# Sum transfers at intervals of their own in each stage, and the first wide layer's second product swept over 26 tiles

## The chip, the cores and the metric

One core of a Trainium2 chip runs the whole kernel. The metric is the device time of one execution in microseconds. The engines are TensorE (PE; its weight loads are shown apart as PEld), VectorE (DVE), ScalarE (ACT), GpSimd (POOL) and SyncE (SP), which issues most transfers.

## What is computed

Two residual layers over 512 tokens of width 1024, in float32, each an attention and then a wide layer (a squared-ReLU MLP with 4096 hidden columns):

```python
def sq_relu_mlp(h, w_up, w_down):
    u = jax.nn.relu(h @ w_up)
    return (u * u) @ w_down

for layer in range(2):
    hn = rmsnorm(h, norm_mix[layer])
    if layer % 2 == 0:
        h = h + hybrid_attention(hn, ...)        # 8 heads GQA and 8 heads MLA, softmax over 512 tokens
    else:
        h = h + neighbourhood_attention(hn, ...) # 16 heads over a window of 8 x 16 tokens
    h = h + sq_relu_mlp(rmsnorm(h, norm_ffn[layer]), ffn_w_up[layer], ffn_w_down[layer])
return rmsnorm(h, final_norm)
```

## The kernel before

Activations stand transposed: hT holds 8 tiles of 128 features by 512 tokens. Every matrix product is made as three products of a high and a low part (hi x hi, hi x lo, lo x hi), so each weight chunk is loaded (raw), its high part made on ScalarE (whi, L236 or L336 or L1340) and its low part as a difference on VectorE (wlo, L226 or L337 or L1341), before TensorE can use it.

The hidden width of a wide layer is 32 tiles of 128. They are treated in three groups, by the constants FIRST, RAW, MORE = 6, 22, 4:

- The first 6 tiles are made by a plain product (`plain`, matmuls of 512 columns on L545 to L547), and their part of the second product is plain too (`gens`).
- The other 26 are made by block products (class `Seven`, L416 to L418): two by two, with seven instead of eight half-size products of 256 columns. The sums of weight blocks that this needs are made on POOL (L329 to L331).
- Of those 26, 22 go on to the second product in the same block form, in three sweeps over 11 pairs of tiles (class `Sweeps`, L1443 to L1445, 256 columns). The last pair or two run as a tail, bank by bank, and the sums are added into hT on VectorE (L1449).
- The last 4 (MORE) are split and used in a plain product at the end (L545 to L547, and in the first layer L1519 for the additions into hT); in the second layer this end also makes the kernel's output.

The sweeps need sums of blocks of w_down. These are made ahead of time in DRAM by transfers alone (class `SumsAhead`): for each pair two copies of 512 KB issued by ScalarE (L841), and four adds of 256 KB issued by POOL (L832), each add a transfer that accumulates into the copy. `steps` yields after each transfer. A small pacemaker sets their place in the program: `tick(us)` is called with the nominal time of each matmul group and each attention step, and whenever `beat["every"]` of it has passed, one more transfer is written into the program. At the end of the block products `drain` writes what is left. `beat` is set when each attention begins to make the sums for the wide layer behind it (in the first attention at its step 22), and held until that layer's block products end.

The order of instructions on an engine is the scheduler's, from the program's order and its own model of times; the second attention alone (`fixed_order`) is in the written order. SP's loads go ahead as far as their buffers are free. In the wide layers one of the raw buffers is `shared`, which the attentions use for their softmax rows.

After the first wide layer the second attention begins: hT is scaled and split tile by tile (`split_g`: L551 on ScalarE, L552 on VectorE), its squares are summed (L559, L561), and TensorE makes the first group of values (`valuesC`, L1657 to L1659: four chunks of tokens, first over hT tiles 0 to 3, then over 4 to 7) and the first queries and keys (`projC`, L545 to L547). The column sums for the norm (L566) and the chain of small operations behind them (L568 to L1584) come beside these.

`bias_rows` writes the position bias of the second attention to DRAM by SP transfers; a step of it stands at every fourth matmul group of the later sweeps.

## Time and profile before

| | us |
|---|---|
| median of three runs | 1173.42 |
| lowest and highest | 1171.39, 1175.44 |
| the profiled execution | 1173.18 |
| its span, first to last instruction | 1171.4 |
| TensorE busy in the span | 1144.9 |

The stages in the trace, on its own time scale from the span's start: the first attention until about 253, its output product to 275, the first wide layer's plain part to about 365, its block products to 467, its sweeps to 578, its plain end to 600, the second attention and its products to about 815, the second wide layer from there to the end (block products to about 1025). A row of a view that groups by stage gives the busy time of each engine in that stretch; the length less TensorE's time is TensorE's idle time. In a row of waits stand the engine, the tile and line that waited, the one waited for, and the total, the count and the longest. In the chain of work that ended last a row is a start, a length and what it was.

### The profile page before, as it was taken

How to read it: one execution, taken by the hardware profiler on the slowest of the kernel's cores; microseconds unless marked ns; L12 is line 12 of the kernel's file. 1: busy time of each engine (PE TensorE's matmuls, PEld its weight loads, DVE VectorE, ACT ScalarE, POOL GpSimd, SP SyncE). 2: the span in 40 equal slices, each digit the busy share in tenths (PEclk: the TensorE clock that was granted, in tenths of full speed). 3: DMA queues.
4: the chain of work that ended last, by engine and by line, in shares of the span. 5: the costliest groups of instructions: out<-in, count | busy, mean ns of one | idle time of the engine just before them, and what ended most of it. 6: DMA issues, size and time to landing. Idle time of an engine off the chain costs nothing.

```text
span 1171.4 us, 20855 instructions
## 1 busy us (share of the span) xinstructions
PE 1144.9 (98%) x7596; PEld 1029.6 (88%) x7596; DVE 919.4 (78%) x1617; ACT 668.2 (57%) x1147; POOL 463.6 (40%) x486
## 2 busy tenths in 40 slices
PE   9989999999999999999999999999999999999996
PEld 8667778888799999999988998988788999999995
DVE  5788988778978787998474676767896878799845
ACT  5468576664536656756253555645552665675625
POOL 3267253333668795000002243333185898600000
PEclk9999999999999999999999999999999999999999
DMA  7123467664577666768426497778566666765702
GB/s 273 55 79 84 122 147 202 176 143 129 114 172 196 162 149 198 234 215 278 131 82 163 131 247 190 191 189 209 178 128 183 170 166 158 193 208 174 249 2 72
DMA packets 129543, 191.55 MB, mean 164 GB/s; under 512 B 12659, under 2 KB 81184, under 8 KB 128736
## 3 DMA queue, kind: packets, MB, share of 16 engines
q1 hardware_dynamic: 112304, 136.61, 37.1%
q0 software_dynamic: 14976, 29.38, 15.5%
q10 hardware_dynamic: 2160, 24.22, 6.2%
q8 instruction: 60, 0.98, 0.4%
q14 instruction: 43, 0.35, 0.1%
HBM read 167.75 MB, written 52.43 MB: 188 GB/s over the span
## 4 chain that ended last, share of the span: by engine, by line
PE 79%; DVE 10%; DMA 4%; ACT 3%; issue 2%; POOL 1%; SPq 0%; DVEq 0%; POOLq 0%; ACTq 0%
PE mm L547 7%; PE mm L545 7%; PE mm L546 7%; PE t L1444 3%; PE t L1443 2%; PE t L1445 2%; PE mm L418 2%; PE mm L416 2%; PE mm L417 2%; PE s L1070 2%; PE o L1058 2%; PE mm L1445 2%; PE mm L1443 2%; PE mm L1444 2%; PE t L1045 2%
## 5 line engine op out<-in xcount | busy, mean ns | idle before, releaser
L545 PE MATMUL mm<-a,whi 128*128 128x512 f32 x407 | 164.8, 407 | 0.3 <-ACT whi L236 0.2
L547 PE MATMUL mm<-a,wlo 128*128 128x512 f32 x407 | 160.2, 395 | 1.6 <-DVE wlo L226 1.5
L546 PE MATMUL mm<-a,whi 128*128 128x512 f32 x407 | 160.9, 395 | 0.1
L337 DVE TENSOR_TENSOR wlo<-raw,whi 128x896 fp32r<-128x896 f32 x80 | 110.5, 1388 | 28.6 <-ACT whi L336 28.4
L236 ACT ACTIVATE whi<-raw 128x1024 fp32r<-128x1024 f32 (+3 forms) x86 | 80.4, 939 | 86.4 <-PE s L546 29.7
L226 DVE TENSOR_TENSOR wlo<-raw,whi 128x1024 fp32r<-128x1024 f32 (+4 forms) x83 | 99.2, 1197 | 36.1 <-ACT whi L236 34.4
L336 ACT ACTIVATE whi<-raw 128x896 fp32r<-128x896 f32 x80 | 75.4, 949 | 83.6 <-PE o L546 22.9
L547 PEld LDWEIGHTS mm<-a,wlo 128*128 128x128 f32 x407 | 76.4, 188 | 19.4 <-DVE wlo L226 3.0
L545 PEld LDWEIGHTS mm<-a,whi 128*128 128x128 f32 x407 | 76.5, 188 | 16.1 <-ACT whi L236 1.3
L546 PEld LDWEIGHTS mm<-a,whi 128*128 128x128 f32 x407 | 76.8, 189 | 14.1 <-DVE a L903 0.4
L1609 POOL DMA_DIRECT2D a<-a x16 | 8.7, 545 | 185.7 <-PE mm L546 169.2
L1078 POOL TENSOR_SCALAR shared<-shared,ti 128x512 f32<-128x512 f32 x64 | 48.3, 758 | 84.5 <-DVE ti L1077 53.5
L418 PE MATMUL mm<-a,wlo 128*128 128x256 f32 x280 | 78.8, 282 | 0.7 <-DVE wlo L337 0.7
L417 PE MATMUL mm<-a,whi 128*128 128x256 f32 x280 | 78.5, 280 | 0.0
L416 PE MATMUL mm<-a,whi 128*128 128x256 f32 x280 | 78.4, 280 | 0.0
L1444 PE MATMUL t<-a,whi 128*128 128x256 f32 x264 | 74.2, 281 | 0.6 <-DVE a L1389 0.5
L1443 PE MATMUL t<-a,whi 128*128 128x256 f32 x264 | 73.9, 280 | 0.0
L1445 PE MATMUL t<-a,wlo 128*128 128x256 f32 x264 | 73.9, 280 | 0.0
L1701 POOL TENSOR_SCALAR shared<-shared,ti 128x256 f32<-128x256 f32 x64 | 35.5, 566 | 95.9 <-DVE ti L1700 83.6
L330 POOL TENSOR_TENSOR raw<-raw 128x512 f32<-128x512 f32 x40 | 67.8, 1695 | 3.1
L1341 DVE TENSOR_TENSOR wlo<-a,whi 128x1024 fp32r<-128x1024 f32 x42 | 51.1, 1221 | 19.4 <-ACT whi L1340 19.4
L329 POOL TENSOR_TENSOR raw<-raw 128x256 f32<-128x256 f32 x40 | 45.1, 1127 | 44.0 <-DMA raw<-in_ffn_w_up_dram 26.1
(399 smaller groups left out, 4007.3 us busy)
## 6 DMA issues: line engine op xcount, KB each, us to landing
made<-in_ffn_w_down_dram ACTq DMA_DIRECT2D x44, 512.0 KB
raw<-in_ffn_w_up_dram SPq DMA_DIRECT2D x80, 256.0 KB
a<-made SPq DMA_DIRECT2D x70, 256.0 KB
made<-in_ffn_w_down_dram POOLq DMA_DIRECT2D x44, 256.0 KB, 6.1
made<-made POOLq DMA_DIRECT2D x44, 256.0 KB, 6.8
raw<-in_ffn_w_down_dram SPq DMA_DIRECT2D x36, 256.0 KB
raw<-in_ffn_w_down_dram SPq DMA_DIRECT2D x16, 512.0 KB
raw<-in_od_w_qkv_dram SPq DMA_DIRECT2D x64, 128.0 KB
```

The source lines that it names most:

```text
L226: z = lambda: (eng or DVE).tensor_tensor(to, src, f32(high), op=ALU.subtract)
L236: ACT.activation(hi[:, 0:m], raw[:, 0:m], AF.Copy)
L337: DVE.tensor_tensor(lo[:, 0:896], raw[:, 128:1024], f32(hi[:, 0:896]), op=ALU.subtract)
L416: PE.matmul(o, wh, x[:, 0], start=kp == 0 and n in (0, 1, 3, 5), stop=False, skip_group_check=True)
L417: PE.matmul(o, wh, x[:, 1], start=False, stop=False, skip_group_check=True)
L418: PE.matmul(o, wl, x[:, 0], start=False, stop=kp == self.np - 1, skip_group_check=True)
L545: PE.matmul(o, wh, xh, start=first, stop=False)
L546: PE.matmul(o, wh, xl, start=False, stop=False)
L547: PE.matmul(o, wl, xh, start=False, stop=last)
L1443: PE.matmul(o, wh, x[:, 0], start=first and m % 2 == 0, stop=False, skip_group_check=True)
L1444: PE.matmul(o, wh, x[:, 1], start=False, stop=False, skip_group_check=True)
L1445: PE.matmul(o, wl, x[:, 0], start=False, stop=last, skip_group_check=True)
```

## The change

Four things:

- RAW and MORE are given per layer: in the first wide layer 26 and 0, in the second 22 and 4 as before. The first layer's second product is thus 6 plain tiles and three sweeps over 13 pairs, and has no plain end; the sums of two more pairs are made ahead for it (52 adds and 26 copies, in place of 44 and 22).
- The interval of the sum transfers was 4.2 from the first attention to the end of the first layer's block products, and 4.4 for the second. It is now 2.8 in the first attention, 3.3 in the plain part of the first wide layer and 5.4 beside its block products; 3.2, 3.6 and 7.0 for the second.
- A step of the bias rows stands at every fifth matmul group of the sweeps, in place of every fourth.
- Where there are no MORE tiles, no product for them is planned.

```diff
-    FIRST, RAW, MORE = 6, 22, 4
+    FIRST, RAW, MORE = 6, (26, 22), (0, 4)
...
-            beat.update(every=4.2, work=ahead0.steps())
+            beat.update(every=2.8, work=ahead0.steps())
...
-    ahead0, ahead1 = (SumsAhead(ins["ffn_w_down"][l], FIRST, RAW // 2) for l in range(2))
+    ahead0, ahead1 = (SumsAhead(ins["ffn_w_down"][l], FIRST, RAW[l] // 2) for l in range(2))
...
         wide[0], LOAD[0] = 4, 7
+        beat["every"] = (3.3, 3.6)[l]
...
         reserve[0] = 3
+        beat["every"] = (5.4, 7.0)[l]
         sweeps = []

-        R = stage(0, RAW + MORE, 0, lambda: sweeps.append(Sweeps(w, FIRST, made)))[1]
-        R, more = R[: RAW // 2], R[RAW // 2 :]
-        V = [Slot() for _ in range(MORE)]
+        R = stage(0, RAW[l] + MORE[l], 0, lambda: sweeps.append(Sweeps(w, FIRST, made)))[1]
+        R, more = R[: RAW[l] // 2], R[RAW[l] // 2 :]
+        V = [Slot() for _ in range(MORE[l])]
...
-            gens = [product(w, FIRST + RAW, up, tiles(512 * c, 512), lambda j, b, c=c: ev(4 * c + j, b))
-                    for c in range(2)]
+            gens = [product(w, FIRST + RAW[l], up, tiles(512 * c, 512), lambda j, b, c=c: ev(4 * c + j, b))
+                    for c in range(2) if up]
...
-            if kind and n % 4 == 0:
+            if kind and n % 5 == 0:
                 next(bias, None)
...
-    beat.update(every=4.4, work=ahead1.steps(), rest=True)
+    beat.update(every=3.2, work=ahead1.steps(), rest=True)
```

The lines behind the edits are numbered one or two higher in the changed kernel (L1657 becomes L1659, L1701 L1703).

Where the transfers stand by the order of the two programs, as copies on ScalarE and adds on POOL:

| | before | now |
|---|---|---|
| first attention (copies before ScalarE's last softmax row, adds before POOL's last one) | 12, 13 | 16, 20 |
| adds beside the first layer's block products | 23 | 20 |
| second attention (likewise) | 10, 13 | 14, 18 |
| adds beside the second layer's block products | 23 | 15 |

TensorE at the end of the first wide layer, before: the last rows of the plain end (o is a bank, a_905 and a_906 are hidden tiles), then the first values of the second attention (a_1081 is the split hT tile 0).

```order
L545 MATMUL o_1080_6750<-a_905_5215,whi_1075_6715 128x512
L546 MATMUL o_1080_6750<-a_905_5215,whi_1075_6715 128x512
L547 MATMUL o_1080_6750<-a_905_5215,wlo_1076_6716 128x512
L545 MATMUL o_1080_6750<-a_906_5216,whi_1075_6715 128x512
L546 MATMUL o_1080_6750<-a_906_5216,whi_1075_6715 128x512
L547 MATMUL o_1080_6750<-a_906_5216,wlo_1076_6716 128x512
L1657 MATMUL s_1090_6828<-whi_1093_6841,a_1081_6803 128x256
L1658 MATMUL s_1090_6828<-wlo_1094_6842,a_1081_6803 128x256
```

The same engine now, where the first values chunk (whi_1105) ends and the second (whi_1107) begins, 48 rows behind the last sweep matmul (a_1096 is hT tile 3, a_1097 tile 4).

```order
L1659 MATMUL s_1102_6954<-whi_1105_6967,a_1096_6932 128x256
L1660 MATMUL s_1102_6954<-wlo_1106_6968,a_1096_6932 128x256
L1661 MATMUL s_1102_6954<-whi_1105_6967,a_1096_6932 128x256
L1659 MATMUL o_1101_6953<-whi_1107_6971,a_1097_6933 128x256
L1659 MATMUL s_1102_6954<-whi_1107_6971,a_1097_6933 128x256
L545 MATMUL mm_1133_7147<-a_1093_6929,whi_1109_6975 128x512
L1660 MATMUL o_1101_6953<-wlo_1108_6972,a_1097_6933 128x256
L1661 MATMUL o_1101_6953<-whi_1107_6971,a_1097_6933 128x256
```

The sweeps' last matmul is now followed directly by the values; the scheduler has pulled one high product each of the other bank and of the first keys (mm_1133) ahead of the first use of wlo_1108.

VectorE at the same place before, from the plain end's last additions into hT (L1519) on; the low parts of the values' weights (L226) stand between them.

```order
L226 TENSOR_TENSOR wlo_1096_6846<-raw_1091_6830,whi_1095_6845 128x1024
L1519 TENSOR_TENSOR hT_74<-hT_74,s_1077_6747 128x512
L1519 TENSOR_TENSOR hT_74<-hT_74,t_1078_6748 128x512
L552 SCALAR_TENSOR_TENSOR a_1085_6807<-hT_74,gT_75,a_1085_6807 128x512
L1519 TENSOR_TENSOR hT_74<-hT_74,t_1079_6749 128x512
L552 SCALAR_TENSOR_TENSOR a_1086_6808<-hT_74,gT_75,a_1086_6808 128x512
L561 TENSOR_TENSOR shared_72<-shared_72,sc_1102_6872 128x512
L1519 TENSOR_TENSOR hT_74<-hT_74,o_1080_6750 128x512
L552 SCALAR_TENSOR_TENSOR a_1087_6809<-hT_74,gT_75,a_1087_6809 128x512
L226 TENSOR_TENSOR wlo_1098_6850<-raw_1091_6830,whi_1097_6849 128x1024
```

And now, from the sweeps' last additions into hT (L1449, bank t_908) on.

```order
L1449 TENSOR_TENSOR hT_74<-hT_74,o_910_5232 128x2x256
L552 SCALAR_TENSOR_TENSOR a_1097_6933<-hT_74,gT_75,a_1097_6933 128x512
L1449 TENSOR_TENSOR hT_74<-hT_74,t_908_5230 128x2x256 x2
L552 SCALAR_TENSOR_TENSOR a_1095_6931<-hT_74,gT_75,a_1095_6931 128x512
L552 SCALAR_TENSOR_TENSOR a_1096_6932<-hT_74,gT_75,a_1096_6932 128x512
L552 SCALAR_TENSOR_TENSOR a_1098_6934<-hT_74,gT_75,a_1098_6934 128x512
L552 SCALAR_TENSOR_TENSOR a_1099_6935<-hT_74,gT_75,a_1099_6935 128x512
L552 SCALAR_TENSOR_TENSOR a_1100_6936<-hT_74,gT_75,a_1100_6936 128x512
L226 TENSOR_TENSOR wlo_1108_6972<-raw_1103_6956,whi_1107_6971 128x1024
L226 TENSOR_TENSOR wlo_1110_6976<-raw_1103_6956,whi_1109_6975 128x1024
L561 TENSOR_TENSOR shared_72<-shared_72,sc_1112_6992 128x512
```

The low part of the second values chunk stands behind six low parts of hT tiles, and all but one of the sums of squares (L561) behind that.

POOL at the end of the second attention before, from the last softmax rows (L1701) on, with the adds that follow; L362 is the second wide layer's first sum of tokens.

```order
L1701 TENSOR_SCALAR shared_72<-shared_72,ti_1475_9106 128x256
L1701 TENSOR_SCALAR shared_72<-shared_72,ti_1476_9108 128x256
L832 DMA made_126_615<-made_126_615 128x512
L1701 TENSOR_SCALAR shared_72<-shared_72,ti_1488_9169 128x256
L1701 TENSOR_SCALAR shared_72<-shared_72,ti_1489_9171 128x256
L832 DMA made_126_615<-in_ffn_w_down_dram 128x512 x2
L832 DMA made_126_615<-made_126_615 128x512 x2
L362 TENSOR_TENSOR a_1560_9526<-a_1559_9523 128x512
```

POOL there now.

```order
L832 DMA made_126_615<-in_ffn_w_down_dram 128x512
L1703 TENSOR_SCALAR shared_72<-shared_72,ti_1500_9303 128x256
L1703 TENSOR_SCALAR shared_72<-shared_72,ti_1501_9305 128x256
L832 DMA made_126_615<-in_ffn_w_down_dram 128x512
L832 DMA made_126_615<-made_126_615 128x512 x2
L832 DMA made_126_615<-in_ffn_w_down_dram 128x512 x2
L832 DMA made_126_615<-made_126_615 128x512
L362 TENSOR_TENSOR a_1572_9662<-a_1571_9659 128x512
```

Six adds in place of four stand between the last softmax row and the wide layer's first sum. On ScalarE the two copies nearest to this place stood among the last softmax rows before, and now stand together behind the high part of the last output weights.

## The prediction

> **What bounds the kernel now.** I read the page's first part, then the busy time of each engine by stage, then what TensorE waits for.

> ```profile
> span 1171.4 us, 20855 instructions
> PE 1144.9 (98%) x7596; PEld 1029.6 (88%) x7596; DVE 919.4 (78%) x1617; ACT 668.2 (57%) x1147; POOL 463.6 (40%) x486
> ```

> TensorE is busy for 98% of the span, so the question for every edit is: does it change TensorE's work, or one of the short waits in its 2%? The stages show where those lie. A row is a stretch of the span, its length, then the busy time of PE, PEld, DVE, ACT and POOL, the granted clock, the DMA engines' share and GB/s.

> ```profile
> 130.00:250.00 120.00, 117.22 (x696) 98.36 (x695) 102.24 (x230) 83.64 (x179) 52.37 (x66) 1.00 0.66 171
> 275.00:365.00 90.00, 89.27 (x510) 77.54 (x509) 74.48 (x90) 41.90 (x60) 57.53 (x55) 1.00 0.62 150
> 365.00:467.00 102.00, 100.98 (x848) 100.20 (x848) 82.65 (x86) 61.87 (x77) 82.10 (x67) 1.00 0.68 171
> 467.00:578.00 111.00, 109.92 (x932) 109.46 (x931) 94.88 (x159) 64.26 (x99) 0.00 (x0) 1.00 0.68 222
> 600.00:640.00 40.00, 39.83 (x229) 34.60 (x228) 22.22 (x48) 14.59 (x24) 4.79 (x10) 1.00 0.46 122
> 677.00:805.00 128.00, 127.84 (x786) 113.24 (x785) 87.12 (x242) 72.70 (x176) 48.68 (x81) 1.00 0.75 195
> 805.00:830.00 25.00, 24.38 (x116) 19.19 (x115) 18.21 (x29) 13.58 (x23) 3.91 (x5) 1.00 0.87 267
> 830.00:945.00 115.00, 114.71 (x706) 102.09 (x705) 95.72 (x117) 58.35 (x83) 77.81 (x66) 1.00 0.63 161
> 945.00:1020.00 75.00, 73.95 (x623) 73.50 (x622) 63.36 (x65) 44.40 (x54) 63.86 (x52) 1.00 0.68 165
> ```

> Length less PE's time is PE's idle time. In the first attention with sum transfers (130 to 250) it is 2.8 us; in the second (677 to 805) 0.2. In the first wide layer it is 0.7 in the plain part (275 to 365), 1.0 beside the block products, 1.1 in the sweeps; in the second 0.6 at its start (805 to 830), 0.3 and 1.1. What ends TensorE's waits beside the block products of both layers, and in the first layer's sweeps:

> ```profile
> PE mm L418 <- DVE wlo L337: 0.5, 1, 0.5
> PE s L418 <- DVE wlo L337: 0.4, 1, 0.4
> PE s L418 <- DVE wlo L337: 0.9, 1, 0.9
> PE mm L418 <- DVE wlo L337: 0.2, 1, 0.2
> PE mm L1445 <- DVE wlo L1341: 0.5, 1, 0.5
> PE t L1444 <- DVE a L1389: 0.5, 1, 0.5
> ```

> All are low parts of weights or tokens that VectorE made late. So the kernel is TensorE's stream of matmuls, with 1 us here and there to be had.

> **The change, part by part.** *The plain end goes, the sweeps take its four tiles.* TensorE loses 96 matmuls of 512 columns (4 tiles, 8 output tiles, 3 products) and gains two pairs of 7 x 4 x 3 = 84 matmuls of 256 columns, 168. Three starts bound both in the trace:

> ```profile
> 467.49 0.28 PE L1443 MATMUL t<-a,whi 128*128 128x256 f32 x1
> 577.56 0.39 PE L545 MATMUL mm<-a,whi 128*128 128x512 f32 x1
> 599.88 0.28 PE L1657 MATMUL s<-whi,a 128*128 128x256 f32 x1
> ```

> The plain end ran from 577.56 to 599.88: 22.3 us for 96, 0.2325 each. The sweeps ran from 467.49 to 577.56: 110.07 us for 11 x 84 = 924, waits included, 0.1191 each; 168 more are 20.0. The term is 22.3 - 20.0 = **-2.3 us**. Halving the width costs nearly nothing a column by these rows. [...]

> *The next layer now starts straight behind the sweeps.* Before, the plain end covered VectorE's and ScalarE's work on the first half of hT. The order now puts on VectorE, behind the sweeps' last matmul, in a row: the last additions into hT, six low parts of the split tokens, and only then the low part of the second values chunk (wlo_1108). The price of each:

> ```profile
> L226 DVE TENSOR_TENSOR wlo<-raw,whi 128x1024 fp32r<-128x1024 f32 x9 | 11.0, 1221 | 8.9 <-ACT whi L236 7.4 <-DMA raw<-in_od_w_qkv_dram 1.5
> L552 DVE SCALAR_TENSOR_TENSOR a<-hT,gT,a 128x512 fp32r<-128x512 f32 x8 | 6.0, 745 | 0.0
> L561 DVE TENSOR_TENSOR shared<-shared,sc 128x512 f32<-128x512 f32 x7 | 4.8, 686 | 0.2
> L1449 DVE TENSOR_TENSOR hT<-hT,t 128x512 f32<-128x512 f32 x4 | 2.7, 684 | 1.5 <-PE t L1445 1.5
> L236 ACT ACTIVATE whi<-raw 128x1024 fp32r<-128x1024 f32 x9 | 9.4, 1057 | 19.7 <-PE t L1444 10.0 <-issue 5.6 <-PE s L546 4.2
> L551 ACT ACTIVATE a<-hT,gT 128x512 fp32r<-128x512 f32 x8 | 5.7, 716 | 3.8 <-DVE hT L1519 3.8
> L559 ACT ACTIVATE sc<-hT 128x512 f32<-128x512 f32 x7 | 4.3, 619 | 0.0
> 608.37 0.95 PE L566 MATMUL t<-ones,shared 128*128 128x1 f32 x8
> ```

> Let 0 be the end of the last sweep matmul's slot. Matmuls of the tail end in groups of 12 (1.4 us), and VectorE follows them without a pause from the second group's end at -5.5: nine operations of 0.68 to 0.75 bring it to 0.9, two additions to 2.3, five low parts (L552) to 6.0, wlo_1108 to 7.2. TensorE has until then 48 matmuls of the first chunk, two of the second and one of the key product: 50 x 0.119 + 0.23 = 6.2. It waits **1.1**. Then 46 matmuls and three of 512 columns bring TensorE to the column sums (L566) at 7.3 + 5.5 + 0.7 = 13.5. VectorE still has before them two low parts of weights (2.4) and six additions (4.1), and in the middle waits for ScalarE, whose eleven operations from 1.0 on (two L236, two L551, six L559, one L236) end at 9.4: it is done at 9.4 + 1.2 + 5 x 0.69 = 14.1. Second wait **0.6**. Together **+1.7**; were VectorE a little earlier 0.3, and 3 if each stands one operation of 1.2 later. The idle time there before was 0.2.

> With four tiles fewer to split in the sweeps' start, VectorE has four operations less there; the wait on L1389 of 0.5 may go: **-0.3** (0 to -0.5).

> *The intervals.* What one transfer occupies:

> ```profile
> q0 software_dynamic: 14976, 29.38, 15.5%
> q10 hardware_dynamic: 2160, 24.22, 6.2%
> made<-in_ffn_w_down_dram ACTq DMA_DIRECT2D x44, 512.0 KB
> made<-in_ffn_w_down_dram POOLq DMA_DIRECT2D x44, 256.0 KB, 6.1
> made<-made POOLq DMA_DIRECT2D x44, 256.0 KB, 6.8
> ```

> The shares are of all 16 engines over 1171.4 us: 181.6 us for 88 adds (at most 2.1 us each, since the key copies share that queue), 72.6 for 44 copies (1.65 each). By the order, the first attention now holds 16 copies and 20 adds in place of 12 and 13, the second 14 and 18 in place of 10 and 13; beside the block products stand 20 adds in place of 23 (two more pairs are to be summed) and 15 in place of 23.

> Beside block products and the plain part before them all idle time is 0.7 + 1.0 + 0.3 + 1.1 = 3.1, the most that there is to gain; in proportion to the adds taken away (13% and 35%) it would be 0.7. I take **-1.0**. In the first attention 25 transfers stood beside 2.8 us of idle time, 0.11 each at most; 11 more are +1.2 at most, and by the second attention's 0.2 us nearly nothing. The order of TensorE's rows is shuffled there too, so it can also fall by a microsecond. I take **+0.5**.

> At the start of the second wide layer the first weights cannot load before the attention gives up its buffer (shared), and the chain of waits runs through that load:

> ```profile
> 807.82 16.77 DMA shared<-in_ffn_w_up_dram
> 824.70 1.07 ACT whi L236
> 825.79 1.23 DVE wlo L226
> ```

> 16.8 us, while four adds and two copies were in flight (805 to 830: DMA share 0.87). The order now has six adds there and the two copies later, on ScalarE behind the last output weights. Nobody's instruction waits on POOL, but the load does on the engines: between 0 and two adds and two copies, 2 x 2.1 + 2 x 1.65 = 7.5 us. The earlier copies are gone from there, so I take the low end: **+0.8**.

> Sum: -2.3 + 1.7 - 0.3 - 1.0 + 0.5 + 0.8 = -0.6. The profiled execution took 1173.18 us, 0.2 under the median of the three; 1172.6 is the forecast.

> **The rivals.** *Faster: the transfers cost more than their idle time in proportion.* All 3.1 us beside the block products and the 0.6 at the second layer's start go, nothing is added in the attentions, and the wait of 1.7 is halved by ScalarE running ahead: -2.3 + 0.8 - 0.3 - 3.1 - 0.6 = -5.5, 1167.7. For it: the longest single waits (0.9) stand where raw loads land late. Against: 20 of the adds are still there in the first layer. Chance 0.25.

> *Slower: the first weights of the second wide layer.* If the two copies and two more adds all go ahead of the load, it lands 7.5 us later and TensorE waits for all of that, since it waits already: -0.6 - 0.8 + 7.5 = +6.1, 1179.3; with the adds alone (4.2) 1176.0. It decides from 4.9 us of delay, that is from a landing at 829.6 on the old time scale. For it: a DMA share of 0.87. Against: the adds stand a little earlier than before. [...] Chance 0.16.

> *Slower by the weight loads.* Each matmul loads its weights, and a load is shown with 188 ns:

> ```profile
> L545 PEld LDWEIGHTS mm<-a,whi 128*128 128x128 f32 x407 | 76.5, 188 | 16.1 <-ACT whi L236 1.3
> ```

> If the narrow ones went at that pace, 168 x 0.188 - 22.3 = +9.3, 1184.1 with the other terms. [...] Chance 0.02.

> *The intervals do nothing.* The adds beside block products fall from 23 to 20 only; with all interval terms at nought it is -2.3 + 1.7 - 0.3 = -0.9, 1172.3. Chance 0.12, on the side of no change.

> **How the numbers follow.** About 0.3% (3.5 us) is what a measurement of this kernel can tell from no change. The forecast's own case has 0.45, and with the intervals that do nothing 0.57 falls within 0.3%. Faster 0.25; slower 0.16 + 0.02 = 0.18. The range reaches down to the faster rival, 1167.5, and up to the middle of the late load's two ends, 1177.5, and leaves a tenth on each side.

> **What would show it.** The plain stretch of 22.3 us is gone and the first layer's sweeps are 130 us long instead of 110. Behind them TensorE waits about 1 us for wlo (L226) and half a microsecond before L566; if neither is there, the second term is wrong. Idle time beside the block products falls from 1.0 and 1.1 but not to nothing. In the second layer the load of shared lands within 2 us of the old time relative to the attention's end; if TensorE's first wait on wlo there is over 4 us, the slower rival has it. A first attention with over 5 us of idle time would make the interval term wrong.

## The result, and the profile after

| | before | after |
|---|---|---|
| median of 17 runs each | 1174.15 us | 1178.33 us |
| lowest and highest | 1170.97, 1176.56 | 1174.61, 1181.92 |
| ratio, with its 95% interval | | 1.0035 (1.0023 to 1.0046) |
| the profiled span | 1171.4 us | 1175.0 us |

The change costs 4.1 us, where 1172.6 was forecast with a range up to 1177.5. TensorE is busy as long as before (1145.0 for 1144.9), though the first layer's sweeps and plain end became 3.4 us shorter, waits included: some of the busy time is work at half pace, below. The profile after, first part:

```profile
span 1175.0 us, 21065 instructions
PE 1145.0 (97%) x7668; PEld 1033.8 (88%) x7668; DVE 917.2 (78%) x1627; ACT 673.8 (57%) x1157; POOL 467.3 (40%) x494
```

The stages after, in the columns of the prediction's table (length, then busy time of PE, PEld, DVE, ACT and POOL, clock, DMA share, GB/s), each stretch moved to where its work now lies:

```profile
130.00:253.00 123.00, 118.81 (x699) 99.04 (x698) 102.52 (x233) 84.67 (x180) 57.28 (x76) 1.00 0.81 199
277.00:367.00 90.00, 89.94 (x517) 78.50 (x516) 73.90 (x89) 42.29 (x60) 65.58 (x58) 1.00 0.66 161
367.00:468.00 101.00, 100.35 (x845) 99.73 (x844) 84.11 (x95) 63.58 (x80) 78.07 (x62) 1.00 0.59 155
597.00:637.00 40.00, 39.72 (x229) 34.24 (x228) 27.70 (x55) 18.46 (x31) 4.54 (x9) 1.00 0.46 122
674.00:802.00 128.00, 127.84 (x788) 113.30 (x787) 87.18 (x244) 72.81 (x176) 52.97 (x88) 1.00 0.84 220
802.00:832.00 30.00, 24.35 (x117) 19.27 (x115) 23.49 (x36) 16.79 (x27) 4.41 (x6) 0.98 0.83 231
832.00:838.00 6.00, 6.00 (x16) 4.75 (x17) 3.96 (x15) 0.00 (x0) 0.00 (x0) 0.51 0.53 178
950.00:1024.00 74.00, 73.40 (x617) 72.92 (x616) 59.31 (x66) 44.40 (x54) 52.47 (x43) 1.00 0.47 135
```

TensorE's idle time fell in the plain part (0.7 to 0.1) and beside the block products (1.0 to 0.7, 1.1 to 0.6), as intended. It rose in the first attention (2.8 to 4.2), and at the start of the second wide layer to 5.7, from 0.6 in the 25 us that the prediction shows. Behind that stand 6 us in which TensorE counts as busy but was granted a clock of 0.51.

Where the time went can be read more sharply from the same matmul's start in both traces. The differences, place by place:

| place | forecast | by the two traces |
|---|---|---|
| first attention and its output product | +0.5 | +2.4 |
| plain part and block products, both layers | -1.0 | -2.2 |
| sweeps and plain end, first layer | -2.3 - 0.3 | -3.4 |
| start of the second attention behind the sweeps | +1.7 | +0.1 |
| second attention | 0 | -0.1 |
| start of the second wide layer | +0.8 | +7.2 |
| sum | -0.6 | +4.0 |

Among the waits at that start, from 820 to 840, are these (engine and tile waiting, what for: total, count, longest):

```profile
PE t L566 <- DVE shared L561: 4.6, 1, 4.6
ACT whi L236 <- DMA shared<-in_ffn_w_up_dram: 4.3, 1, 4.3
PE mm L545 <- ACT whi L236: 0.8, 1, 0.8
```

TensorE waits 4.6 us before the column sums of the norm (L566), for the last sum of squares on VectorE. The load itself is hardly longer than before (16.77): in the chain of waits after,

```profile
804.91 17.84 DMA shared<-in_ffn_w_up_dram
```

### The profile page after: what moved, and what is told of

Same layout as the page of the kernel before. It is cut to its first block, busy times and chain, and to the rows that moved or that the text cites. A ratio compares the mean times of both kernels' runs of the same rounds, so it can differ in the third digit from the quotient of the medians.

```text
span 1175.0 us, 21065 instructions
## 1 busy us (share of the span) xinstructions
PE 1145.0 (97%) x7668; PEld 1033.8 (88%) x7668; DVE 917.2 (78%) x1627; ACT 673.8 (57%) x1157; POOL 467.3 (40%) x494
## 4 chain that ended last, share of the span: by engine, by line
PE 77%; DVE 5%; DMA 5%; issue 1%; ACT 0%; POOL 0%; SPq 0%; DVEq 0%; ACTq 0%; POOLq 0%
PE mm L547 6%; PE mm L545 6%; PE mm L546 6%; PE mm L418 3%; PE mm L416 3%; PE mm L417 3%; PE t L1443 3%; PE t L1445 3%; PE t L1444 3%; DMA a<-a 2%; PE mm L1445 2%; PE mm L1443 2%; PE t L416 2%; PE mm L1444 2%; PE t L417 2%; PE t L418 2%
## 5 line engine op out<-in xcount | busy, mean ns | idle before, releaser
L545 PE MATMUL mm<-a,whi 128*128 128x512 f32 x395 | 160.9, 409 | 3.7 <-ACT whi L236 1.9
L547 PE MATMUL mm<-a,wlo 128*128 128x512 f32 x395 | 156.7, 399 | 0.3 <-DVE wlo L226 0.3
L546 PE MATMUL mm<-a,whi 128*128 128x512 f32 x395 | 156.6, 396 | 0.1
L337 DVE TENSOR_TENSOR wlo<-raw,whi 128x896 fp32r<-128x896 f32 x80 | 109.8, 1377 | 27.9 <-ACT whi L336 27.3
L236 ACT ACTIVATE whi<-raw 128x1024 fp32r<-128x1024 f32 (+3 forms) x82 | 76.3, 933 | 75.6 <-PE s L546 26.9
L226 DVE TENSOR_TENSOR wlo<-raw,whi 128x1024 fp32r<-128x1024 f32 (+4 forms) x79 | 94.3, 1195 | 30.7 <-ACT whi L236 30.4
L545 PEld LDWEIGHTS mm<-a,whi 128*128 128x128 f32 x395 | 74.8, 189 | 20.2 <-ACT whi L236 3.0
L546 PEld LDWEIGHTS mm<-a,whi 128*128 128x128 f32 x395 | 74.9, 190 | 13.2 <-DVE a L588 0.4
L1341 DVE TENSOR_TENSOR wlo<-a,whi 128x1024 fp32r<-128x1024 f32 x54 | 66.4, 1232 | 25.1 <-ACT whi L1340 25.0
L1443 PE MATMUL t<-a,whi 128*128 128x256 f32 x288 | 80.8, 281 | 0.0
L1444 PE MATMUL t<-a,whi 128*128 128x256 f32 x288 | 80.8, 280 | 0.0
L1445 PE MATMUL t<-a,wlo 128*128 128x256 f32 x288 | 80.7, 280 | 0.0
L418 PE MATMUL mm<-a,wlo 128*128 128x256 f32 x280 | 78.8, 281 | 1.0 <-DVE wlo L337 1.0
L1340 ACT ACTIVATE whi<-a 128x1024 fp32r<-128x1024 f32 x54 | 56.9, 1054 | 37.4 <-PE t L1444 30.4
L1703 POOL TENSOR_SCALAR shared<-shared,ti 128x256 f32<-128x256 f32 x64 | 34.7, 557 | 92.3 <-DVE ti L1702 79.8
L330 POOL TENSOR_TENSOR raw<-raw 128x512 f32<-128x512 f32 x40 | 63.0, 1575 | 3.1
## 6 DMA issues: line engine op xcount, KB each, us to landing
made<-in_ffn_w_down_dram ACTq DMA_DIRECT2D x48, 512.0 KB
a<-made SPq DMA_DIRECT2D x86, 256.0 KB
raw<-in_ffn_w_up_dram SPq DMA_DIRECT2D x80, 256.0 KB
made<-in_ffn_w_down_dram POOLq DMA_DIRECT2D x48, 256.0 KB, 5.9
made<-made POOLq DMA_DIRECT2D x48, 256.0 KB, 6.0
raw<-in_ffn_w_down_dram SPq DMA_DIRECT2D x32, 256.0 KB
a<-in_ffn_w_down_dram SPq DMA_DIRECT2D x32, 256.0 KB
```

What stands on the lines that cost most here:

```text
L226: z = lambda: (eng or DVE).tensor_tensor(to, src, f32(high), op=ALU.subtract)
L236: ACT.activation(hi[:, 0:m], raw[:, 0:m], AF.Copy)
L337: DVE.tensor_tensor(lo[:, 0:896], raw[:, 128:1024], f32(hi[:, 0:896]), op=ALU.subtract)
L418: PE.matmul(o, wl, x[:, 0], start=False, stop=kp == self.np - 1, skip_group_check=True)
L545: PE.matmul(o, wh, xh, start=first, stop=False)
L546: PE.matmul(o, wh, xl, start=False, stop=False)
```

## The experiments

Ratios are to the kernel before on the same chip, with 95% intervals of about 0.0013 to each side. A difference between two of them is uncertain by 0.0018, some 2 us.

**1. The column sums later.** In the changed kernel the sums stood behind only 8 matmuls of the first weights, before behind 32. The first theory was that this place alone lets TensorE run into the wait. From n == 9 TensorE keeps the written order, and the norm is written behind 33 matmuls:

```diff
+                if l == 1 and n == 9:
+                    pe = tc.manual_schedule(engines={mybir.EngineType.PE})
+                    pe.__enter__()
-                if n == (11 if l == 0 else 13):
+                if n == (11 if l == 0 else 10):
                     norm()
+                if l == 1 and n == 10:
+                    pe.__exit__(None, None, None)
```

> The changed kernel, with one thing moved on TensorE: the four column sums of the second wide layer (L566) are held to their written place, behind 33 matmuls of the first weights instead of 8. All sum transfers, copies and loads stand where the changed kernel has them. Theory "place" (TensorE, which runs in order, comes to the sums before the eight squares are there, and loses 4.6 us of waiting and some 3 us of half pace behind it): 33 matmuls of 0.2325 are 7.7 us, which cover the 4.6, so the wait before L566 falls under 1 us, the loss between 820 and 840 from 9.2 to 2 or 3, and the time by 6 to 7, from 1178.3 to about 1171.5, a ratio to the kernel before of 0.997 to 0.999. Theory "late load" (the adds crowd the load of shared, and TensorE lacks the first weights themselves): the place decides nothing, the wait moves to the first low parts, and the ratio stays at 1.0025 to 1.0045.

1178.0 us, ratio 1.0043 (1.0028 to 1.0059): nothing gained. The theory of the place fell, and so, at first sight, the late load had it. TensorE's longest wait from 818 on, and VectorE's timeline there (start, length, what):

```profile
PE mm L547 <- DVE wlo L226: 5.8, 1, 5.8
```

```profile
826.96 0.75 DVE L552 SCALAR_TENSOR_TENSOR a<-hT,gT,a 128x512 fp32r<-128x512 f32 x1 [2.07 <-ACT a L551]
...
831.42 0.68 DVE L561 TENSOR_TENSOR shared<-shared,sc 128x512 f32<-128x512 f32 x1
832.02 2.35 DVE L226 TENSOR_TENSOR wlo<-shared,whi 128x1024 fp32r<-128x1024 f32 x2
```

The wait moved to the first low part of the weights. That is no late load: ScalarE's two high parts were made from 824.3 on, a microsecond each, and the low part needs 1.2 us. It begins at 832.0, directly behind eight operations on token tiles 4 to 7 (L552, L561) that stand ahead of it in VectorE's row. The same operations also end in the last square that L566 waits for. So the next theory was VectorE's row. VectorE's timeline before:

```profile
825.79 1.23 DVE L226 TENSOR_TENSOR wlo<-shared,whi 128x1024 fp32r<-128x1024 f32 x1 [3.13 <-ACT whi L236]
...
829.33 0.74 DVE L552 SCALAR_TENSOR_TENSOR a<-hT,gT,a 128x512 fp32r<-128x512 f32 x1
...
833.78 0.68 DVE L561 TENSOR_TENSOR shared<-shared,sc 128x512 f32<-128x512 f32 x1
```

And after:

```profile
825.51 0.75 DVE L552 SCALAR_TENSOR_TENSOR a<-hT,gT,a 128x512 fp32r<-128x512 f32 x1 [1.65 <-ACT a L551]
...
829.97 0.69 DVE L561 TENSOR_TENSOR shared<-shared,sc 128x512 f32<-128x512 f32 x1
830.57 2.36 DVE L226 TENSOR_TENSOR wlo<-shared,whi 128x1024 fp32r<-128x1024 f32 x2
```

Before, the low part goes first, and TensorE has 32 matmuls to do while the squares are summed. After, the low part begins 4.8 us later than before, though on ScalarE the high parts begin 1.85 earlier (822.85 for 824.70):

```profile
822.85 2.01 ACT L236 ACTIVATE whi<-shared 128x1024 fp32r<-128x1024 f32 x2 [4.28 <-DMA shared<-in_ffn_w_up_dram]
```

**2. The same place, in the kernel before.** Column sums (`compact_r`) behind 9 first-weight matmuls there, what follows them (`norm_rest`) where it was, TensorE in written order in between:

```diff
+            if l == 1:
+                pe = tc.manual_schedule(engines={mybir.EngineType.PE})
+                pe.__enter__()
...
+                if l == 1 and n == 2:
+                    r = compact_r(acc)
+                if l == 1 and n == 13:
+                    norm_rest(r)
+                if l == 1 and n == 13:
+                    pe.__exit__(None, None, None)
```

> The kernel before, with one thing moved on TensorE: the same four column sums held behind 9 matmuls of the first weights instead of 32; those matmuls stand in their written order. Transfers, intervals and the plain end are as before. Theory "place": TensorE reaches the sums at about 828.5 (first weights at 825.8, 0.5 of wait, 9 x 0.2325), the last square is summed at 833.9: 5 us of wait, and about 3 us of half pace behind it, so 1180 to 1183, a ratio of 1.005 to 1.008, though no transfer has moved. Theory "late load": nothing in the load has changed, so within 0.5 us of the kernel before, a ratio of 0.999 to 1.001.

1181.6 us, ratio 1.0073 (1.0058 to 1.0089), with `PE t L566 <- DVE shared L561` at 5.1 us. VectorE's row is as before there, with the low part first (`DVE wlo L226 <- ACT whi L236`, 4.6 us at the longest: it is the high part that it waits for). So the place of the sums alone is enough for a loss, with every transfer where it was; experiment 1 says that it isn't the only way to it.

**3. Without the intervals.** The changed kernel with 4.2 and 4.4 throughout:

```diff
-            beat.update(every=2.8, work=ahead0.steps())
+            beat.update(every=4.2, work=ahead0.steps())
-        beat["every"] = (3.3, 3.6)[l]
+        beat["every"] = (4.2, 4.4)[l]
-        beat["every"] = (5.4, 7.0)[l]
+        beat["every"] = (4.2, 4.4)[l]
-    beat.update(every=3.2, work=ahead1.steps(), rest=True)
+    beat.update(every=4.4, work=ahead1.steps(), rest=True)
```

> The changed kernel with every interval put back to the old ones (4.2 from the first attention on, 4.4 from the second): only the sweeps over 26 tiles and the missing plain end are left of the change. Its order has the column sums of the second wide layer behind 32 matmuls again. Theory "place": the sweeps gain 2.3 (22.3 us of plain end against 168 x 0.1191), the start of the second layer's attention costs nothing to 1.7, so 1171.5 to 1173.5, a ratio of 0.998 to 1.000, with no loss above 3 us between 820 and 840. Rival "the missing plain end is what costs": 1176 or more, 1.002 or more.

1169.7 us, ratio 0.9968 (0.9958 to 0.9979), better than was expected. The missing plain end, together with the bias rows' wider step and the two more pairs of sums, is a gain of 3.8 us, so the intervals cost the whole loss and this gain on top.

**4. The second layer's intervals put back** (3.6, 7.0 and 3.2 to 4.4; the first layer's stay):

```diff
-        beat["every"] = (3.3, 3.6)[l]
+        beat["every"] = (3.3, 4.4)[l]
-        beat["every"] = (5.4, 7.0)[l]
+        beat["every"] = (5.4, 4.4)[l]
-    beat.update(every=3.2, work=ahead1.steps(), rest=True)
+    beat.update(every=4.4, work=ahead1.steps(), rest=True)
```

> The changed kernel with the second layer's intervals put back to 4.4 (attention, plain part and block products); the first layer's stay at 2.8, 3.3 and 5.4, and the plain end is gone. Column sums of the second wide layer behind 32 matmuls. Theory "place": as without the plain end alone, plus what the first layer's intervals do (the first attention's losses of 140 to 220 us are 3 us larger in the changed kernel than before, those beside the block products 1.5 us smaller): 1171.5 to 1174.5, a ratio of 0.998 to 1.0005. Rival "the first layer's intervals cost as much as the second's": 1176 or more.

1172.7 us, ratio 0.9987 (0.9975 to 1.0000): the second layer's intervals cost 0.0048 (5.6 us). The first layer's cost 0.0019 beside experiment 3, which is about the uncertainty of such a difference.

**5. The low part first.** Changed kernel; VectorE is held to the written order from token tile 4 on, with the first weights asked for there:

```diff
+        first = len(asked)
+        four = product(w, 0, xp, tiles(0, 512), lambda j, b: ev(j, b), lambda n: [mmb(), mmb(), mmb(), sbk()])
         for k in range(KD):
+            if l == 1 and k == 4:
+                dve = tc.manual_schedule(engines={mybir.EngineType.DVE})
+                dve.__enter__()
+                weights(first, 0)
             split_g(hT[:, k, :], gffn(l, k), X[k].pair())
             sumsq_acc(k, acc, DVE)
+        if l == 1:
+            dve.__exit__(None, None, None)
```

> The changed kernel, with one thing moved on VectorE: the low part of the first weights of the second wide layer (L226, wlo from shared) is held ahead of the splits and squares of token tiles 4 to 7 (eight operations of L552 and L561), where the kernel before has it. The column sums come to stand behind 32 first-weight matmuls by themselves. Loads, adds and copies up to there are those of the changed kernel. Holding the column sums back alone changed nothing: TensorE then waited 5.75 us at the first low part instead. Theory "VectorE's row" (in the changed kernel the low part is made 6.7 us after its high part, though it needs only 1.2, since eight operations stand ahead of it; both rows of TensorE wait for the end of that row): low part done at about 825.3, waits there of 1 to 1.5 in all, no half pace, loss between 820 and 840 of 2 to 3.5 instead of 9.2, so 1170.5 to 1172.5, a ratio of 0.9965 to 0.9990. Theory "late load": the load lands no earlier, so the loss stays and the ratio is 1.0025 to 1.0045.

1171.7 us, ratio 0.9992 (0.9983 to 1.0001), 0.0043 (5.0 us) less than the changed kernel; the ratio is just above the expected range. By the starts of the same matmuls 8.1 us are gone between 822 and 847. VectorE's low part with the first of the eight operations behind it, and all that is left of TensorE's waits there:

```profile
828.61 1.22 DVE L226 TENSOR_TENSOR wlo<-shared,whi 128x1024 fp32r<-128x1024 f32 x1
830.17 0.75 DVE L552 SCALAR_TENSOR_TENSOR a<-hT,gT,a 128x512 fp32r<-128x512 f32 x1 [0.34 <-ACT a L551]
```

```profile
PE mm L545 <- ACT whi L236: 0.8, 1, 0.8
```

**6. The low part last, in the kernel before.** VectorE keeps the written order from token tile 4 until the first weights have been asked for, so the eight operations come first and the low part behind them:

```diff
+            if l == 1 and k == 4:
+                dve = tc.manual_schedule(engines={mybir.EngineType.DVE})
+                dve.__enter__()
...
+                if l == 1 and n == 0:
+                    dve.__exit__(None, None, None)
```

> The kernel before, with the same operation moved the other way: the low part of the first weights of the second wide layer behind the splits and squares of token tiles 4 to 7, as the changed kernel has it. The column sums come to stand behind 8 first-weight matmuls by themselves. Nothing else of the change is in it. Theory "VectorE's row": it loses what the changed kernel loses there, 4.5 to 5.5 us of waiting and about 2.5 of half pace: 1180 to 1183, a ratio of 1.005 to 1.008. Theory "late load": as the kernel before, 0.999 to 1.001.

1179.3 us, ratio 1.0058 (1.0043 to 1.0072). TensorE's wait, and VectorE's low part behind the eight:

```profile
PE t L566 <- DVE shared L561: 5.2, 1, 5.2
```

```profile
830.90 2.35 DVE L226 TENSOR_TENSOR wlo<-shared,whi 128x1024 fp32r<-128x1024 f32 x2
```

One row moved on VectorE, none of the change, and by the starts of the same matmuls 6.8 us are lost there, nearly the 7.2 of the changed kernel. With 5, this shows VectorE's row to be the cause; in 5 and 6 the place of the column sums followed it by itself (32 and 8 matmuls). Experiments 1 and 2 moved one of the two alone: with the low part late the loss stays though the sums are late, and with the sums early it comes though the low part is early.

**7 and 8. The first attention.** Experiment 7 is experiment 3 with one number changed, 8 is experiment 5 with the same number changed back. The edit of 7:

```diff
-            beat.update(every=4.2, work=ahead0.steps())
+            beat.update(every=2.8, work=ahead0.steps())
```

The same two lines the other way round are the edit of 8.

> The changed kernel with all intervals put back but the first attention's 2.8 (then 4.2 from the first wide layer's start, 4.4 in the second layer): beside the kernel that has no interval changed and no plain end (1169.7), one number differs, 2.8 for 4.2. The two traces of before and after put the first attention's cost at 2.3 us, by the same matmuls' starts (2.4 later at 268 where nothing was later at 128). Theory "the close transfers delay the raw loads and the key copies": 1171.5 to 1173, a ratio of 0.9980 to 0.9995. As priced in the prediction (+0.5): 1170.2, a ratio of 0.9965 to 0.9975.

> The changed kernel with two repairs: the low part of the first weights held ahead on VectorE as above, and the first attention's interval back at 4.2. All other intervals are the changed kernel's. If the two costs are what they seem (7.4 and 2.3), it comes to 1178.3 - 9.7 = 1168.6, a ratio of 0.994 to 0.997, at or below the kernel with the plain end alone removed (1169.7). If the cost is the transfers as such, 1173 or more.

Experiment 7: 1173.4 us, ratio 1.0014 (1.0001 to 1.0027), 0.0046 more than experiment 3, beyond the expected range. Experiment 8: 1167.0 us, ratio 0.9959 (0.9944 to 0.9973), 0.0033 less than experiment 5, and faster than both kernels. TensorE's waits on weights, tokens and key copies in the first attention, before, after, and in 7:

```profile
PE mm L545 <- ACT whi L236: 0.2, 1, 0.2
```

```profile
PE mm L545 <- DVE a L988: 1.5, 3, 1.0
PE mm L545 <- ACT whi L236: 1.1, 1, 1.1
PE s L1070 <- DMA a<-a: 0.5, 1, 0.5
```

```profile
PE mm L545 <- DVE a L988: 1.7, 3, 1.2
PE s L1070 <- DMA a<-a: 1.5, 1, 1.5
PE mm L545 <- ACT whi L236: 1.1, 1, 1.1
```

Other waits there, for low parts of the softmax rows (L1048), fell from 2.2 us to 0.7. The first two kinds are alike in every trace with 2.8 (1.1 to 1.8 and 1.0 to 1.1) and at most 0.2 with 4.2; that they come with the order that the scheduler makes for it is likely, but no run holds that order apart from the interval. The third, a copy of keys inside SBUF, was 0.5 to 3.3 us in the seven traces with 2.8; of the eight with 4.2 it shows in two, with 0.2 (experiment 2) and 0.7 (8). The DMA engines are busier there (0.81 for 0.66), but that the copy waits for that reason is argued, not shown. Experiment 5's trace had the longest:

```profile
PE s L1070 <- DMA a<-a: 3.3, 1, 3.3
```

**9. Filling the wait.** Changed kernel with 20 products of ones, 40 matmuls in the trace, where TensorE stands still (`idle_work(20, stb())` ahead of `compact_r`, second layer only).

> The changed kernel with 20 matmuls of ones (128 columns, into a bank that nothing reads) ahead of the column sums of the second wide layer, where TensorE waits 4.6 us for the squares. They stand behind the 8 first-weight matmuls and ahead of L566 on TensorE; at the 0.223 us that such a pair took at the kernel's start at full pace they fill 4.5 us. Nothing becomes ready any earlier. If the half pace behind the wait is a price of its own for TensorE standing still, it goes: the 512-column matmuls behind L566 keep 0.23 us, and the time falls by 2.5 to 3 to 1175.5, a ratio of 1.000 to 1.0025, with the same squares and low part ending the wait. If the half pace comes from something else (late operands, the DMA engines), the ratio stays at 1.0025 to 1.0045.

1176.8 us, ratio 1.0031 (1.0017 to 1.0046): above what was expected, and in time inconclusive. In the trace the half pace at the second wide layer's start is gone and the matmuls behind stand 2.3 us earlier, but its first attention had 3.1 us of waits for key copies, and the mean clock of the whole trace was 0.993, where the kernel before had 0.998. At the second wide layer's start TensorE waited 0.2 us before the sums and 1.4 for the high part, at a clock of 1.00.

**10. An interval of 3.4 for 3.2 in the second attention**, nothing else:

```diff
-    beat.update(every=3.2, work=ahead1.steps(), rest=True)
+    beat.update(every=3.4, work=ahead1.steps(), rest=True)
```

> The changed kernel with the second attention's interval at 3.4 in place of 3.2. There is one add less between the last softmax and the layer, and the two copies stand some rows earlier; the order that comes out has the low part of the first weights ahead of the splits of tiles 4 to 7 again, and the column sums behind 32 matmuls. Theory "VectorE's row": the whole loss at the second wide layer's start goes though the transfers stand nearly as close: 1170.5 to 1172.5, a ratio of 0.9965 to 0.9990, as with the low part held by hand. Theory "the close transfers": 17 adds for 18 are worth a tenth of it at most, 1177 or more, 1.002 or more.

1172.0 us, ratio 0.9985 (0.9973 to 0.9997), 0.0050 (5.9 us) below the changed kernel for two tenths of a microsecond. The order puts the low part first again, and it is made at 825.17 where the changed kernel makes it at 830.57:

```profile
825.17 1.23 DVE L226 TENSOR_TENSOR wlo<-shared,whi 128x1024 fp32r<-128x1024 f32 x1 [3.73 <-ACT whi L236]
```

By the orders alone (not run) there is no trend in it: with 3.0, 3.6, 4.0 and 4.4 the low part comes first, with 3.2 and 3.8 it comes last.

**11. Both attentions' intervals put back**, the others as changed:

```diff
-            beat.update(every=2.8, work=ahead0.steps())
+            beat.update(every=4.2, work=ahead0.steps())
-    beat.update(every=3.2, work=ahead1.steps(), rest=True)
+    beat.update(every=4.4, work=ahead1.steps(), rest=True)
```

> The changed kernel with both attentions' intervals back at 4.2 and 4.4; the intervals beside the plain part (3.3, 3.6) and beside the block products (5.4, 7.0) are the changed kernel's. Column sums behind 32 matmuls. Beside the kernel with no plain end and no interval changed (1169.7) only these two stages differ, so it prices the wider intervals beside the block products, which the prediction put at -1.0: 1168 to 1169.5, a ratio of 0.995 to 0.997. If the wider intervals do nothing, 0.9965 to 0.998.

1169.1 us, ratio 0.9964 (0.9952 to 0.9976). Beside experiment 3 that is 0.0004 less, too little to tell in time; by the two traces the same matmuls are 1.0 earlier at the block products' end and 1.9 at the end of all.

**12 and 13. The price of standing still, without the close transfers of the first attention.** 12 is the changed kernel with 4.2 there, 13 has the products of ones as well.

> The changed kernel with only the first attention's interval back at 4.2. The second wide layer's start is the changed kernel's: low part behind eight operations, column sums behind 8 matmuls. The loss there (9.2 in the slice 820 to 840) stays, the first attention's goes: 1178.3 less 3 to 5 is 1173.5 to 1175.5, a ratio of 0.9995 to 1.002; against the kernel that also has the low part first (1167.0, 0.9959) it prices VectorE's row at 0.0045 to 0.0065. Its first attention has no long wait for key copies, so its times should spread less than the changed kernel's 7 us.

> The same kernel with the 20 matmuls of ones ahead of the column sums. With the first attention at 2.8 the filled wait showed no half pace in its trace (the matmuls behind it stood 2.4 us earlier than in the changed kernel's trace), yet the median gained 1.6 at most, inside the spread of the first attention. Here that spread is gone. If standing still has a price of its own: 2 to 2.5 below the kernel without the filling, a ratio lower by 0.0017 to 0.0022. If not, the two ratios are within 0.0008.

Experiment 12: 1175.6 us, ratio 1.0022 (1.0009 to 1.0035), just above what was expected, and its times still spread by 5.8 us (the changed kernel's by 7.3, those of the kernel before by 6.0 in the same runs): the first attention is not what spreads them most, as had been thought. Experiment 13: 1173.3 us, 1.0004 (0.9992 to 1.0017). The stretches from 829 in 12, then in 13 (the clock stands behind the five busy times):

```profile
829.00:832.00 3.00, 3.00 (x11) 2.61 (x12) 2.96 (x6) 0.00 (x0) 0.00 (x0) 0.50 0.42 126
832.00:835.00 3.00, 3.00 (x10) 2.38 (x9) 1.68 (x12) 0.00 (x0) 0.00 (x0) 0.65 0.67 225
```

```profile
829.00:832.00 3.00, 2.76 (x19) 2.35 (x19) 3.00 (x4) 0.56 (x1) 0.00 (x0) 1.00 0.00 0
832.00:835.00 3.00, 3.00 (x15) 2.41 (x14) 2.73 (x13) 0.09 (x1) 0.00 (x0) 1.00 0.68 251
```

Work without a use, in a wait that stays as long, makes the kernel 2.1 us faster (0.0018, no more than the uncertainty of such a difference); by the starts of the same matmuls it is 2.4, and the clock of the two traces agrees with half pace as the cause. Of the 7.2 us lost at the second wide layer's start, about 2.4 are thus half pace and 4.8 waiting. Between 12 and 8, which differ in VectorE's row alone, lie 0.0063, or 7.4 us.

## Why the prediction was wrong, point by point

**The step that failed** is the start of the second wide layer, "The earlier copies are gone from there, so I take the low end: +0.8", against +7.2. It asked only when the load would land. There it was right: the load took 17.84 us in place of 16.77, though the two copies that the prediction counted as gone were issued at 811.95, inside the load's time. But whoever waits for this load is not TensorE but ScalarE, then VectorE, then TensorE, and the interval had changed VectorE's row: the low part of those weights had moved behind eight operations that start 0.6 us apart. The column sums' move to 8 matmuls follows from that. The prediction laid out VectorE's row behind the first layer's sweeps operation by operation, and did not do it here.

**The slower rival** gave 1176.0 to 1179.3, which holds 1178.3, but for a cause that the runs refute. It wanted a landing after 829.6 on the old time scale; the load landed at 822.75, which is 825.7 there, since its start stood 2.9 us earlier than before. That the time fell into this rival's range is chance. Its sign, a first wait on wlo of over 4 us, did not come; the wait stood before L566. Experiments 2 and 6 make the same loss with no transfer moved.

**The plain end** was right in direction and too small: 132.39 us of sweeps and plain end became 128.94, -3.4 for -2.6. The sweeps' own pace after, from first to last start:

```profile
468.27 0.28 PE L1443 MATMUL t<-a,whi 128*128 128x256 f32 x1
...
597.21 0.28 PE L1659 MATMUL o<-whi,a 128*128 128x256 f32 x1
```

1092 matmuls in 128.94 are 0.1181 each, where 0.1191 had been taken from sweeps that held waits; that is a microsecond. The rival by weight loads (0.188) is out.

**The second attention's start** behind the sweeps was feared too much: no wait of 1.1 for wlo, and 0.23 before L566 (at 609.69) for 0.6. The term came to 0.1 in place of 1.7, below its own lower bound of 0.3: the chain was built from full durations, one behind the other, and had wlo_1108 done 7.2 us behind the sweeps. It was done at 6.0, and the five low parts ahead of it took 3.40 us in place of 5 x 0.745.

**The first attention** was taken as +0.5, at most 1.2, by sharing 2.8 us of idle time among 25 transfers. It cost 2.4 in the traces, and 0.0013 to 0.0046 (1.5 to 5.4 us) in three pairs of kernels (after and 12, 5 and 8, 3 and 7). The mean price of a transfer said nothing of the new waits that come with a closer row: on key copies, on a high part and on tokens.

**Beside the block products** -1.0 was taken, above the 0.7 that the proportion gave, and by the traces -2.2 came; the times (experiment 11 against 3) can't confirm it.

Without the failed step the other places add to -3.2, and with it repaired by hand (experiment 5) the change is worth 0.0008, which the interval does not tell from nothing. What is good in it is the missing plain end and, by the traces alone, the wider intervals; with the low part first and 4.2 in the first attention it makes 0.9959.

## What to carry to other kernels

When a number changes what a scheduler sees, compare every engine's row at each place where something is waited for, not only the row of the waiter and the transfer: here one moved row on VectorE, off any transfer, cost 7 us, and two tenths in the interval put it back. A forecast that names "the load" as the risk should follow the operand through every engine that handles it until TensorE has it. A tuned interval that wins or loses by the order that happens to come out of it should be pinned: hold the critical operation in its place, then tune.

## What the hardware showed

Behind the waits of 4.6 to 5.8 us at the second wide layer's start (4.6 in the changed kernel and in experiment 12, 5.1 in 2, 5.2 in 6, 5.8 in 1) the stretches of these traces show a granted clock of 0.50 for TensorE. In the changed kernel the 512-column matmuls behind came every 0.43 us in place of 0.23, and full pace came back 7.1 us after work had begun again (830.71 to 837.84); by the clock of the stretches it was 5.1 in experiment 1 and 7.5 in 2. From the chain of work after, one of the slow and, from the timeline, the first at full pace again:

```profile
836.37 0.43 PE mm L547
```

```profile
837.87 0.39 PE L545 MATMUL s<-a,whi 128*128 128x512 f32 x1
```

A lower clock stands beside shorter waits too. Experiment 4, with 1.7 us for a key copy in the first attention, was granted 0.99 from 130 to 250, where the kernel before and experiment 3, without that wait, had 1.00. Experiment 5, with 3.3, had a mean of 0.994 over its whole trace, experiment 8, with 0.7, had 0.998.

Cut into these steps, the two traces have three at full pace with 2.4 us of idle time or more: one in the kernel before, near its end (3.0), and two in the changed kernel (3.1, and 2.4 near its end). Half pace followed all three. No other step at full pace had more than 1.9, and full pace followed all of those. The wait of 4.6 us in the changed kernel fell into two steps, 1.5 into the first, which full pace followed, and 3.1 into the second, which half pace followed. Three cases make no rule, but in them half pace went with the idle time inside one step. The second of the two and what came behind it (columns as in the stages above; the clock stands behind the five busy times):

```profile
827.60:831.01 3.41, 0.30 (x3) 0.30 (x3) 3.41 (x6) 2.74 (x5) 0.00 (x0) 1.00 0.00 0
831.01:834.42 3.41, 3.41 (x12) 2.98 (x12) 3.38 (x7) 0.00 (x0) 0.00 (x0) 0.50 0.35 108
834.42:837.84 3.42, 3.42 (x9) 2.64 (x8) 1.58 (x10) 0.00 (x0) 0.00 (x0) 0.50 0.58 204
837.84:841.25 3.41, 3.41 (x16) 2.76 (x15) 1.23 (x1) 1.06 (x1) 0.00 (x0) 1.00 0.00 0
```

At about 73 us there is 2.4 us of idle time in the softmax. In the kernel before 1.9 us of it fall into one step, in experiment 3 2.2:

```profile
69.86:73.27 3.41, 1.51 (x7) 0.92 (x5) 2.99 (x10) 2.40 (x3) 0.58 (x1) 1.00 0.79 259
73.27:76.69 3.42, 2.94 (x13) 2.29 (x14) 3.24 (x11) 2.48 (x7) 0.14 (x1) 1.00 0.03 10
```

```profile
71.08:74.49 3.41, 1.19 (x6) 0.63 (x4) 2.99 (x10) 2.07 (x3) 0.26 (x1) 1.00 0.79 269
74.49:77.91 3.42, 3.26 (x8) 2.58 (x9) 2.90 (x10) 2.33 (x6) 0.00 (x0) 0.50 0.00 0
```

The same idle time was thus followed by half pace in one trace and not in the other, though nothing in experiment 3 touches this place. It may be part of the spread of every kernel's times; that is not tested.

So a wait of 4.6 us cost about half as much again in half pace (2.4 us, by the starts of the same matmuls in experiments 12 and 13), and the matmuls of ones made the kernel 2.1 us faster, which is no more than the uncertainty of such a difference.
